# Batched matmul, one core: the first x in eight strided transfers, and each store queued behind y instead of between x and y

## The chip, the cores and the metric

One core of a Trainium2 chip runs the whole kernel. The metric is the device time of one execution, in microseconds (us). The kernel before takes 263.36 us, the median of three runs (263.03 to 263.59). Its profiled execution has a span of 261.6 us and a mean granted TensorE clock of 0.895.

## What is computed

```python
def setup_inputs():
    batch, m, k, n = 16, 512, 768, 1024
    return {
        "x": np.random.randn(batch, k, m).astype(np.float32),
        "y": np.random.randn(batch, k, n).astype(np.float32),
    }

def reference(x, y):
    return np.einsum('bkm,bkn->bmn', x, y).astype(np.float32)
```

There are sixteen independent products, each of a transposed 768x512 matrix with a 768x1024 matrix, all in float32. The kernel casts both inputs to bfloat16 before it multiplies. One batch needs 1.573 MB of x and 3.146 MB of y from HBM, and it writes 2.097 MB of output.

## The kernel before

One batch is called a round below. There are two buffers for x and two for y (`xs`, `ys` in float32), two slots of bfloat16 copies (`xb`, `yb`), two halves of PSUM (`ps`) and five output buffers (`ob`). All transfers are issued by SyncE, in program order, on one queue. A partition holds six consecutive rows of x or y, so that each partition's share is one contiguous piece of HBM (12 KB of x, 24 KB of y).

```python
    x_v = x.rearrange("b (p ko) m -> b p ko m", ko=KT)      # KT = 6, 128 partitions
    y_v = y.rearrange("b (p ko) n -> b p ko n", ko=KT)
    o_v = out.rearrange("b (p mo) n -> b p mo n", mo=MT)    # MT = 4
    LAG = 4
    NO = 5
    ...
    def wide_dma(key, dst, src, dram_rows, load):
        # the first transfer of a key is an ordinary one with 128 rows;
        # later ones are copies of it whose HBM side is widened:
        # 4 partitions' rows of x, or 2 of y, are one row
        if key not in made:
            made[key] = nc.sync.dma_start(dst, src)
            return made[key]
        ...
    def parts(b):
        return 2 if b in (15,) else 1            # the last y is cast in two halves

    nx = [sum(1 + parts(a) for a in range(b)) + 1 for b in range(B)]

    def store(b):
        if b < B - 2:
            nc.sync.wait_ge(groups, 2 * (b + 2))   # the matmuls of round b+1 are done
        else:
            nc.sync.wait_ge(outs, b - (B - 3))
        nc.sync.dma_start(o_v[b], ob[b % NO][:]).then_inc(so[b % NO], 16)

    for b in range(B):                             # SyncE
        i = b % 2
        if b >= 2:
            nc.sync.wait_ge(cast, nx[b - 2])                  # x of b-2 is cast
        wide_dma("x", xs[i][:], x_v[b], 4, True).then_inc(sx[i], 16)
        if LAG <= b < B - 1:
            store(b - LAG)
        if b >= 2:
            nc.sync.wait_ge(cast, nx[b - 2] + parts(b - 2))   # y of b-2 is cast
        wide_dma("y", ys[i][:], y_v[b], 2, True).then_inc(sy[i], 16)
        if b == B - 1:
            store(b - LAG)
    for b in range(B - LAG, B):
        store(b)
    ...
    for b in range(B):                             # VectorE
        i = b % 2
        n = 16 * (b // 2 + 1)
        if b >= 2:
            nc.vector.wait_ge(groups, 2 * (b - 1))
        nc.vector.wait_ge(sx[i], n)
        nc.vector.tensor_copy(xb[:, i], xs[i][:]).then_inc(cast, 1)
        nc.vector.wait_ge(sy[i], n)
        for h in range(parts(b)):
            ...   # cast of y, whole or in two halves, then_inc(cast, 1)
    ...
            # TensorE: 48 matmuls of 128x128 by 128x512 a round (4 mo x 6 kt x 2 nt);
            # after each half of mo: then_inc(groups, 1)
    ...
    for b in range(B):                             # ScalarE
        if b >= NO:
            nc.scalar.wait_ge(so[b % NO], 16 * (b // NO))
        for g in range(2):
            nc.scalar.wait_ge(groups, 2 * b + g + 1)
            cp = nc.scalar.copy(ob[b % NO][:, g * HB:(g + 1) * HB]..., ps[g][:])
            if b < B - 1:
                cp.then_inc(room, 1)
```

Of the kernel before, what the change touches and what calls it, by code (L numbers as in the profile page):

```python
# [1 line left out]

_os.environ.setdefault("NEURON_RT_ULTRASERVER_MODE", "4")

# [2 lines left out]

# [5 lines left out]


@with_exitstack
def kernel(
    ctx: ExitStack,
    tc: tile.TileContext,
    x: bass.AP,
    y: bass.AP,  # L20
    out: bass.AP,
):
    nc = tc.nc
    P = 128
    FP32 = mybir.dt.float32
    BF16 = mybir.dt.bfloat16

    B, K, M = x.shape
    _, _, N = y.shape
    KT = K // P  # L30
    MT = M // P
    NF = 512
    NT = N // NF

    x_v = x.rearrange("b (p ko) m -> b p ko m", ko=KT)
    y_v = y.rearrange("b (p ko) n -> b p ko n", ko=KT)
    o_v = out.rearrange("b (p mo) n -> b p mo n", mo=MT)

    LAG = 4
    NO = 5
    KH = KT // 2

    ctx.enter_context(tc.tile_critical())
    ec = ctx.enter_context
    xs = [ec(nc.sbuf_tensor(f"xs{i}", [P, KT, M], FP32)) for i in range(2)]
    ys = [ec(nc.sbuf_tensor(f"ys{i}", [P, KT, N], FP32)) for i in range(2)]
    xb = ec(nc.sbuf_tensor("xb", [P, 2, KT, M], BF16))
    yb = ec(nc.sbuf_tensor("yb", [P, 2, KT, N], BF16))  # L50
    ob = [ec(nc.sbuf_tensor(f"ob{i}", [P, MT, N], FP32)) for i in range(NO)]

    HB = MT // 2
    ps = [ec(nc.psum_tensor(f"ps{i}", [P, HB, NT, NF], FP32)) for i in range(2)]
    sx = [ec(nc.semaphore(f"sx{i}")) for i in range(2)]
    sy = [ec(nc.semaphore(f"sy{i}")) for i in range(2)]
    so = [ec(nc.semaphore(f"so{i}")) for i in range(NO)]
    cast = ec(nc.semaphore("cast"))
    ready = ec(nc.semaphore("ready"))
    room = ec(nc.semaphore("room"))  # L60
    groups = ec(nc.semaphore("groups"))
    idle = ec(nc.semaphore("idle"))
    outs = ec(nc.semaphore("outs"))


    made = {}
# [7 lines that stand above are left out]
        pat = mybir.BassSymbolicTensorAccessPattern  # L74
        widen = lambda a: a.rearrange("(q r) k m -> q (r k m)", r=dram_rows)
        plain = lambda a: a.rearrange("p k m -> p (k m)")
        s, d = (widen(src), plain(dst)) if load else (plain(src), widen(dst))
        return nc.sync.add_instruction(_copy.replace(
            made[key].ins, name=nc.get_next_instruction_name(),
            ins=(pat(ap=s.ap, dtype=s.dtype, bass_ap=s, is_dma=False),),  # L80
            outs=(pat(ap=d.ap, dtype=d.dtype, bass_ap=d, is_dma=False),),
            sync_info=None, ant_dge_precooked=False))


    def parts(b):
        return 2 if b in (15,) else 1
# [9 lines that stand above are left out]
            nc.sync.wait_ge(groups, 2 * (b + 2))  # L96
        else:
            nc.sync.wait_ge(outs, b - (B - 3))
        nc.sync.dma_start(o_v[b], ob[b % NO][:]).then_inc(so[b % NO], 16)

    for b in range(B):
        i = b % 2
        if b >= 2:
            nc.sync.wait_ge(cast, nx[b - 2])
        wide_dma("x", xs[i][:], x_v[b], 4, True).then_inc(sx[i], 16)
        if LAG <= b < B - 1:
            store(b - LAG)
        if b >= 2:
            nc.sync.wait_ge(cast, nx[b - 2] + parts(b - 2))
        wide_dma("y", ys[i][:], y_v[b], 2, True).then_inc(sy[i], 16)  # L110
        if b == B - 1:
            store(b - LAG)
    for b in range(B - LAG, B):
        store(b)


    for _ in range(60):
        nc.vector.sem_inc(idle, 1)
    for b in range(B):
        i = b % 2  # L120
        n = 16 * (b // 2 + 1)
        if b >= 2:
            nc.vector.wait_ge(groups, 2 * (b - 1))
        nc.vector.wait_ge(sx[i], n)
        nc.vector.tensor_copy(xb[:, i], xs[i][:]).then_inc(cast, 1)  # L125
        nc.vector.wait_ge(sy[i], n)
        for h in range(parts(b)):
            ks = slice(h * KT // parts(b), (h + 1) * KT // parts(b))
            nc.vector.tensor_copy(yb[:, i, ks], ys[i][:, ks]).then_inc(cast, 1)  # L129


    for b in range(B):
        nc.gpsimd.wait_ge(cast, nx[b]).then_inc(ready, 1)
        for h in range(parts(b)):
            nc.gpsimd.wait_ge(cast, nx[b] + h + 1).then_inc(ready, 2 // parts(b))


    x_w = xb[:].rearrange("p s k (j mo) -> p s k mo j", mo=MT)
    pe = OrderedEngineSet([nc.tensor.engine])
    with nc.Fori(0, B // 2, engines=pe):  # L140
        with nc.Fori(0, 2, engines=pe) as s:
            nc.tensor.wait_ge(ready, 2).then_inc(ready, -2)
            for mo in range(MT):
                g, m = divmod(mo, HB)
                if m == 0:
                    nc.tensor.wait_ge(room, 1).then_inc(room, -1)  # L146
                for kt in range(KT):
                    if mo == 0 and kt == KH:
                        nc.tensor.wait_ge(ready, 1).then_inc(ready, -1)
                    for nt in range(NT):  # L150
                        mm = nc.tensor.matmul(  # L151
                            ps[g][:, m, nt], x_w[:, bass.ds(s, 1), kt, mo],
                            yb[:, bass.ds(s, 1), kt, nt * NF:(nt + 1) * NF],
                            start=(kt == 0), stop=(kt == KT - 1))
                if m == HB - 1:
                    mm.then_inc(groups, 1)


    nc.scalar.nop().then_inc(room, 2)
    for _ in range(60):  # L160
        nc.scalar.sem_inc(idle, 1)
    for b in range(B):
# [4 lines that stand above are left out]
            cp = nc.scalar.copy(ob[b % NO][:, g * HB:(g + 1) * HB].rearrange("p m (t f) -> p m t f", f=NF),  # L167
                                ps[g][:])
            if b < B - 1:
                cp.then_inc(room, 1)  # L170
        if b == B - 2:
            nc.scalar.drain().then_inc(outs, 1)
    cp.then_inc(outs, 1)

    for i in range(NO):
        nc.sync.wait_ge(so[i], 16 * len(range(i, B, NO)))


# [1 line left out]
_INS = ['x', 'y']  # L180
_OUTS = [((16, 512, 1024), 'float32')]


# [23 lines left out]
```

## Time and profile before

| what | from the profile of before |
|---|---|
| TensorE (PE) busy | 190.3 us, 73% of the span, 768 matmuls |
| VectorE (DVE) busy | 82.0 us, 31%: casts of x at 1.76 us, of y at 3.36 us |
| ScalarE (ACT) busy | 61.1 us, 23%: copies out of PSUM at 1.87 us |
| moved by DMA | 75.50 MB read, 33.55 MB written |
| transfers | 16 of x, 16 of y, 16 stores |

The span is one execution as the hardware profiler recorded it. "Busy" is the time in which an engine had an instruction at work. A row of tenths cuts the span into 40 equal slices (6.54 us each) and gives the busy share of each slice as a digit. The DMA row is the mean share over the core's sixteen DMA engines, and the GB/s row is what they moved. An issue line of the transfer queue (SPq) gives the start and the length of the instruction that starts a transfer; the transfer itself comes later. The time from issue to landing ends when the completion semaphore is full.

### The profile page before, as it was taken

The numbers are of one execution on the slowest core, as the hardware profiler recorded it, in microseconds if no ns is written. First come the engines' busy times: TensorE is split into PE (matmuls) and PEld (weight loads), VectorE is DVE, ScalarE is ACT, GpSimd is POOL, SyncE is SP. The second block draws the span as 40 slices with busy tenths as digits, with TensorE's granted clock in tenths as the row PEclk, the third lists the DMA queues.
The fourth block names the chain that finished last, engine by engine and source line by source line (L and its number), as shares of the span: only waits on it lengthen the run. The fifth ranks groups of instructions, "written<-read, shape, count | busy, mean of one in ns | idle before, by whom it ended". The sixth has DMA issues, their size and how long they took to land. (4 is left out here: it accounts for less than half of the span.)

```text
span 261.6 us, 2506 instructions
## 1 busy us (share of the span) xinstructions
PE 190.3 (73%) x768; PEld 90.5 (35%) x768; DVE 82.0 (31%) x33; ACT 61.1 (23%) x33; POOL 0.2 (0%) x4
## 2 busy tenths in 40 slices
PE   0009999995494995939959499694968969499920
PEld 0004555552142352514425134252423525255500
DVE  0261734520705206052160612507043070525000
ACT  1000432343022022220312203222140222214220
POOL 0000000000000000000000000000000000000000
PEclk9999999999589597997989869799795989999995
DMA  6998999999999999989999998999999999999994
GB/s 263 442 485 376 474 398 451 328 466 436 403 443 378 461 443 428 448 371 469 406 476 401 403 504 366 451 466 423 408 393 491 388 441 453 406 411 428 426 391 180
DMA packets 4514, 109.07 MB, mean 417 GB/s; under 512 B 768, under 2 KB 768, under 8 KB 768
## 3 DMA queue, kind: packets, MB, share of 16 engines
q1 hardware_dynamic: 4512, 109.05, 97.9%
q14 instruction: 2, 0.02, 0.0%
HBM read 75.50 MB, written 33.55 MB: 417 GB/s over the span
## 5 line engine op out<-in xcount | busy, mean ns | idle before, releaser
L151 PE MATMUL ps<-yb,xb 128*128 x768 | 190.3, 414 | 59.8 <-PEq L146 59.7
L151 PEld LDWEIGHTS ps<-yb,xb 128*128 x768 | 90.5, 118 | 159.0 <-issue 93.9
L167 ACT COPY ob<-ps 128x2048 f32<-128x2048 f32 x32 | 59.8, 1869 | 185.5 <-PE ps L151 185.5
L129 DVE CAST yb<-ys 128x6144 bf16<-128x6144 f32 (+1 forms) x17 | 53.8, 3172 | 139.6 <-DMA ys<-in_y_dram 139.6
L125 DVE CAST xb<-xs 128x3072 bf16<-128x3072 f32 x16 | 28.2, 1760 | 18.0 <-DMA xs<-in_x_dram 15.0
L167 ACT ACT_TABLE_LOAD x1 | 1.3, 1283 | 5.3 <-issue 5.3
L191 POOL MEMSET const-bfloat16-1.0<- 128x1 bf16 x1 | 0.1, 102 | 0.0
L191 POOL MEMSET const-uint8-127<- 128x1 uint8 x1 | 0.1, 102 | 0.0
L191 POOL MEMSET const-float32-1.0<- 128x1 f32 x1 | 0.1, 99 | 0.0
L191 POOL MEMSET const-float32-0.0<- 128x1 f32 x1 | 0.1, 98 | 0.2 <-issue 0.2
## 6 DMA issues: line engine op xcount, KB each, us to landing
ys<-in_y_dram SPq DMA_DIRECT2D x16, 3072.0 KB, 28.2
out_dram<-ob SPq DMA_DIRECT2D x16, 2048.0 KB, 24.1
xs<-in_x_dram SPq DMA_DIRECT2D x16, 1536.0 KB, 29.8
```

Of the source, the lines that this page charges most:

```text
L125: nc.vector.tensor_copy(xb[:, i], xs[i][:]).then_inc(cast, 1)
L129: nc.vector.tensor_copy(yb[:, i, ks], ys[i][:, ks]).then_inc(cast, 1)
L151: mm = nc.tensor.matmul(ps[g][:, m, nt], x_w[:, bass.ds(s, 1), kt, mo], yb[:, bass.ds(s, 1), kt, nt * NF:(nt + 1) * NF], start=(kt == 0), ...
L167: cp = nc.scalar.copy(ob[b % NO][:, g * HB:(g + 1) * HB].rearrange("p m (t f) -> p m t f", f=NF), ps[g][:])
L191: nc = _bacc.Bacc("TRN2", target_bir_lowering=False, num_devices=1)
```

## The change

Two things are changed in the order of SyncE. The first x is no longer one transfer of 128 partitions but eight transfers of 16 partitions each: transfer c takes partitions c, c+8, c+16 and so on, so that each of the sixteen DMA engines has one partition in each of the eight. It is meant to let all engines start on the first data early. They all count on the semaphore of the first x buffer, which therefore stands 7 x 16 = 112 higher from then on. The first ordinary x transfer, which later ones are copies of, is now that of round 1. And each store now stands behind the y of its round in the queue, and no longer between x and y; this puts the operand that TensorE waits for ahead of the output, which nothing waits for until five rounds later.

```diff
+
+    x_first = x_v[0].rearrange("(a c) k m -> a c k m", c=8)
+    for c in range(8):
+        nc.sync.dma_start(xs[0][c::8], x_first[:, c]).then_inc(sx[0], 16)
     for b in range(B):
         i = b % 2
         if b >= 2:
             nc.sync.wait_ge(cast, nx[b - 2])
-        wide_dma("x", xs[i][:], x_v[b], 4, True).then_inc(sx[i], 16)
-        if LAG <= b < B - 1:
-            store(b - LAG)
+        if b > 0:
+            wide_dma("x", xs[i][:], x_v[b], 4, True).then_inc(sx[i], 16)
         if b >= 2:
             nc.sync.wait_ge(cast, nx[b - 2] + parts(b - 2))
         wide_dma("y", ys[i][:], y_v[b], 2, True).then_inc(sy[i], 16)
-        if b == B - 1:
+        if b >= LAG:
             store(b - LAG)
     for b in range(B - LAG, B):
         store(b)
@@
-        nc.vector.wait_ge(sx[i], n)
+        nc.vector.wait_ge(sx[i], n + (112 if i == 0 else 0))
```

## The prediction

> **What bounds the kernel now.** I read the page's slices and DMA totals first, because they show which resource is never free.
>
> ```profile
> span 261.6 us, 2506 instructions
> ...
> DMA  6998999999999999989999998999999999999994
> ...
> DMA packets 4514, 109.07 MB, mean 417 GB/s; under 512 B 768, under 2 KB 768, under 8 KB 768
> ...
> q1 hardware_dynamic: 4512, 109.05, 97.9%
> ```
>
> The DMA engines are busy for 97.9% of the span. Only the first slice (6) and the last (4) are clearly below 8. So any gain has to come from those two ends, or from a higher rate in between.
>
> For the rate I took the casts in order of time on VectorE, since a cast of y that waited for DMA starts when its data has landed. From round 11 on:
>
> ```profile
> 177.58 3.36 DVE L129 CAST yb<-ys 128x6144 bf16<-128x6144 f32 x1 [10.32 <-DMA ys<-in_y_dram]
> ...
> 193.38 3.36 DVE L129 CAST yb<-ys 128x6144 bf16<-128x6144 f32 x1 [10.33 <-DMA ys<-in_y_dram]
> ...
> 225.18 3.36 DVE L129 CAST yb<-ys 128x6144 bf16<-128x6144 f32 x1 [10.35 <-DMA ys<-in_y_dram]
> ...
> 236.15 3.43 DVE L129 CAST yb<-ys 128x3072 bf16<-128x3072 f32 x2 [5.46 <-DMA ys<-in_y_dram]
> ```
>
> From 177.58 to 225.18 are three rounds, so a round takes 15.87 us. It moves 1.573 + 2.097 + 3.146 = 6.816 MB, which makes 430 GB/s. TensorE needs 12.0 to 13.5 us of such a round, so it waits for y and not the reverse.
>
> Next I asked whether the queue ever runs dry. In the queue's own order of time, a steady round is:
>
> ```profile
> 183.09 0.47 SPq L72 DMA_DIRECT2D xs<-in_x_dram  x1
> 193.73 0.34 SPq L99 DMA_DIRECT2D out_dram<-ob  x1
> 196.77 0.47 SPq L72 DMA_DIRECT2D ys<-in_y_dram  x1
> ```
>
> The median time from issue to landing is 29.8 us for x and 28.2 us for y, nearly two rounds, so about 12 MB stands in the queue. A wait of SyncE on TensorE (130.2 us in all in the queue's waits) costs nothing while that much is queued.
>
> Last, the two ends. At the start, in windows of half a microsecond:
>
> ```profile
> 1.50:2.00 0.50, 0.00 (x0) 0.00 (x0) 0.00 (x0) 0.00 (x0) 0.00 (x0) 1.00 0.59 98
> 2.00:2.50 0.50, 0.00 (x0) 0.00 (x0) 0.00 (x0) 0.00 (x0) 0.00 (x0) 1.00 0.63 123
> 2.50:3.00 0.50, 0.00 (x0) 0.00 (x0) 0.00 (x0) 0.00 (x0) 0.00 (x0) 1.00 0.86 221
> 3.00:3.50 0.50, 0.00 (x0) 0.00 (x0) 0.00 (x0) 0.00 (x0) 0.00 (x0) 1.00 0.69 295
> 3.50:4.00 0.50, 0.00 (x0) 0.00 (x0) 0.00 (x0) 0.00 (x0) 0.00 (x0) 1.00 1.09 467
> ```
>
> The last column is GB/s. The rate climbs for 2 us, from 1.5 to 3.5, before it is full. In those 2 us 0.5 x (98+123+221+295) = 368 KB moved where 860 KB could have, a loss of 1.15 us. I read it as the sixteen engines getting their first work one after the other, the first at about 1.55 and the last near 3.4. At full rate an engine moves 27 GB/s and needs 3.66 us for its 98 KB of x, its eight rows; 3.4 + 3.66 = 7.06, and the first cast indeed starts at 7.11.
>
> At the end, issue plus landing time of the last five stores (windows of the transfer view) gives 241.05, 245.8, 250.7, 255.5 and 260.3. They are 4.8 us apart, and 2.097 MB in 4.8 us is 437 GB/s. So DMA holds the end as well, though the chain that ended last shows TensorE until 250.03 and the last copy until 251.93. The last store was issued at 251.9 and took 8.4 us. Alone it would take some 7.3 us (the first x took 6.1 us alone, of which 3.66 was data; 2.1 MB of data is 4.88 us, plus the same 2.4), so TensorE's chain has only about 1.1 us to spare.
>
> [...]
>
> [...] 48 transfers x 16 = 768, the profile's count of packets under 512 B.
>
> [...] Here the first issue is at 0.95 and the first packets are at about 1.55.
>
> [...] ten gaps of 2.4 to 6.4 us are each followed by 48 matmuls that take 12.0 to 13.5 us, but after the gap of 3.74 us before the last two rounds 96 of them took only 20.91 us.
>
> **The change part by part: the first x.** It removes one transfer and adds eight, 1.573 MB either way. An issue costs 0.34 us (stores) to 0.47 us (wide loads), with 0.05 us between; the first x took 0.39. I take 0.38 + 0.05 = 0.43 us, so the eight occupy SyncE from 0.95 to 4.4, where y of round 0 is issued (before: 1.39). An engine needs 12.3 KB / 27 GB/s = 0.457 us for each row, slightly more than the issue interval, so the rows follow each other without a hole. [...] it shrinks from 2 us to about 2/8 = 0.25, and the last engine starts at about 1.8. The x then lands at about 1.8 + 3.66 + 0.1 = 5.6 instead of 7.1.
>
> This gain is mostly lost again at once. The y of round 0 has 128 rows, and it makes its own climb: first engine at 4.4 + 0.6 = 5.0, last engine at 7.0. The engines have finished x at about 5.3 to 5.5, so the late half of them stand idle. Before, the last engine went over to y at 7.06; now at 7.0. Averaged over the engines, the change goes from (5.2 + 7.06)/2 = 6.1 to about 6.0. I book -0.1 to -0.4 us, and carry it undiminished to the end, because DMA is never idle after this.
>
> Further descriptors: x of round 1 is now the ordinary one (128 rows instead of 32), +96 packets, and seven more transfers make 112 completions; 4512 becomes 4720. That is 13 small extras an engine beside some 282, of the same bytes. I book +0.1 us.
>
> **The change part by part: the stores.** In eleven rounds, b = 4 to 14, two transfers change places: x, store, y becomes x, y, store. As a cycle this is one write of 4.88 us between 11 us of reads in either order, so the number of changes between reading and writing is the same and no byte is added. In the queue before the last five stores stands the same sum of work: y of round 15 should still land near 236.15. What moves is y against x: it lands one store, 4.9 us, earlier in its round. Then y lands 7.3 us behind its x, is cast 3.4 us later, and TensorE works from 11 to 24 us behind x, that is until 8 us into the next round. The new place of the store asks for that very round of matmuls just after the next y was issued, some 11 us into the round; it is met by then and the store goes out immediately. So SyncE no longer waits long for TensorE, and at least st, x, y and st, some 7 MB or 16 us, stay in the queue. The five output buffers also suffice: the store five rounds back lands about 4 us before the x whose matmuls' copy needs it, some 20 us early. Booked: 0.
>
> At the tail, round 14 now computes earlier (its y lands near 220.3), ends at 235 to 236, and TensorE then waits for y of round 15: 236.15 + 1.72 for half a cast + 0.57 of handing over = 238.4, instead of 239.6. With a slow restart it takes 12.2 (up to 13.4) us instead of 10.4: end at 250.6 (251.8) against 250.03. The last store would be issued at 252.5 (253.7), and alone end at 259.8 (261.0), against 260.3 set by DMA. Booked: +0.1 on average.
>
> Sum: -0.25 + 0.1 + 0 + 0.1, in effect nothing: 263.36 - 0.05, with the start perhaps doing better than I booked. I say 263.1 us.
>
> **The rivals.** One: the climb at the start is gone altogether, because issues of 16 rows are far cheaper than 0.43 us and y is queued early. Then up to the 1.15 us lost are won: 262.2. Against it speaks that all issues in the trace, of very different row counts, take 0.34 to 0.58 us. Two: the climb is a fixed delay for each engine, whatever the row count. Then x still lands near 7, y's issue at 4.4 does no harm, and the time is unchanged, 263.4. Three: the slow restart of TensorE at the tail takes the place of DMA as what ends last: +0.7, 264.0. Four: the place of stores against reads changes the rate. Rounds 5 to 7 take 16.2 to 16.7 us where later ones take 15.87, some 1.5 us in all, and I can't name what costs it; it may go or double: 261.9 to 264.9.
>
> **Range and chances.** The certain pieces lie within 0.5 us; the rivals reach from 262 to 264, and the three runs of before are themselves 0.56 apart. The range is 262.0 to 264.2. The border of 2% is 5.3 us away on either side. The gain is limited by 1.15 us at the start[...]; a loss would need the queue to run dry each round. So 0.97 within 2%, 0.015 for each side.
>
> **What would show it right or wrong.** Right: first cast at about 5.6, y of round 0 landing still near 14.8; in steady rounds the store's issue directly behind y's, the idle time before casts of y falling from 10.3 to some 5.5 and before casts of x rising by as much; rounds of 15.87 us; y of round 15 landing at about 236; the last five landings 4.8 us apart; 4720 packets. Wrong: issues of the small transfers much over or under 0.43 us, a DMA share under 0.97, rounds that differ from 15.87 by more than 0.1 us, or a last store issued after 253.

## The result and the profile after

The changed kernel takes 266.34 us (median of 4 runs, 265.98 to 266.74) beside 263.2 us for the kernel before. The ratio is 1.0117, with a 95% interval of 1.0097 to 1.0138. It is slower by 1.2%, or about 3.1 us. The prediction was 263.1 us with a range of 262.0 to 264.2: the change is within the 2% that was given a chance of 0.97, and outside the range.

The page of the changed kernel, its slices and DMA totals:

```profile
span 264.6 us, 2513 instructions
...
DMA  6999998999999899899999999899998999999993
GB/s 154 320 414 489 409 468 364 468 468 389 419 391 505 372 426 478 369 446 421 468 438 426 404 411 486 379 446 451 386 488 379 451 468 434 389 409 426 429 424 129
DMA packets 4722, 109.07 MB, mean 412 GB/s; under 512 B 880, under 2 KB 880, under 8 KB 880
...
q1 hardware_dynamic: 4720, 109.06, 97.7%
```

The same row of the kernel before:

```profile
GB/s 263 442 485 376 474 398 451 328 466 436 403 443 378 461 443 428 448 371 469 406 476 401 403 504 366 451 466 423 408 393 491 388 441 453 406 411 428 426 391 180
```

The engines are as busy as before (97.7%, before 97.9%), and the bytes are the same. But the second slice is a warning: a busy digit of 9 over 320 GB/s, where before it stood over 442. Engines that are busy but move less are not short of work: each packet takes longer (0.93 us instead of 0.457, counted below). The casts of VectorE in order of time show where the time goes:

```profile
11.02 1.76 DVE L128 CAST xb<-xs 128x3072 bf16<-128x3072 f32 x1 [11.02 <-DMA xs<-in_x_dram]
18.85 3.36 DVE L132 CAST yb<-ys 128x6144 bf16<-128x6144 f32 x1 [6.07 <-DMA ys<-in_y_dram]
...
191.32 3.36 DVE L132 CAST yb<-ys 128x6144 bf16<-128x6144 f32 x1 [5.57 <-DMA ys<-in_y_dram]
199.97 1.76 DVE L128 CAST xb<-xs 128x3072 bf16<-128x3072 f32 x1 [5.29 <-DMA xs<-in_x_dram]
207.19 3.36 DVE L132 CAST yb<-ys 128x6144 bf16<-128x6144 f32 x1 [5.46 <-DMA ys<-in_y_dram]
...
239.04 3.43 DVE L132 CAST yb<-ys 128x3072 bf16<-128x3072 f32 x2 [5.59 <-DMA ys<-in_y_dram]
```

The first two casts of the kernel before:

```profile
7.11 1.76 DVE L125 CAST xb<-xs 128x3072 bf16<-128x3072 f32 x1 [7.11 <-DMA xs<-in_x_dram]
15.03 3.36 DVE L129 CAST yb<-ys 128x6144 bf16<-128x6144 f32 x1 [6.16 <-DMA ys<-in_y_dram]
```

The first cast waits until 11.02 us where it waited until 7.11. The y of round 0 is 3.82 us later (18.85 against 15.03), and the last y 2.89 us later (239.04 against 236.15). In the middle a round still takes 15.87 us (207.19 - 191.32). So the loss is there before the first matmul.

The issues on SyncE's queue: the eight transfers and the y behind them, and a store behind y in a steady round.

```profile
0.95 5.04 SPq L104 DMA_DIRECT2D xs<-in_x_dram  x8
6.03 0.58 SPq L72 DMA_DIRECT2D ys<-in_y_dram  x1
...
194.71 0.47 SPq L72 DMA_DIRECT2D ys<-in_y_dram  x1
195.23 0.58 SPq L99 DMA_DIRECT2D out_dram<-ob  x1
```

In windows of the start, whose last two columns are the busy share of the DMA engines and GB/s:

```profile
2.00:2.50 0.50, 0.00 (x0) 0.00 (x0) 0.00 (x0) 0.00 (x0) 0.00 (x0) 1.00 0.53 147
2.50:3.00 0.50, 0.00 (x0) 0.00 (x0) 0.00 (x0) 0.00 (x0) 0.00 (x0) 1.00 0.77 246
3.00:3.50 0.50, 0.00 (x0) 0.00 (x0) 0.00 (x0) 0.00 (x0) 0.00 (x0) 1.00 1.32 393
...
5.00:6.00 1.00, 0.00 (x0) 0.00 (x0) 0.00 (x0) 0.66 (x1) 0.00 (x0) 1.00 0.98 209
...
7.00:8.00 1.00, 0.00 (x0) 0.00 (x0) 0.00 (x0) 0.00 (x0) 0.00 (x0) 1.00 1.00 205
8.00:9.00 1.00, 0.00 (x0) 0.00 (x0) 0.00 (x0) 0.00 (x0) 0.00 (x0) 1.00 0.97 197
```

A packet counts in the window in which it starts. By 3.5 us the changed kernel has started on 0.5 x (147 + 246 + 393) = 393 KB, hardly more than the 368 KB of before. From 5 to 9 us it moves 197 to 246 GB/s, about half of the 430 of a steady round, with a busy share near 1. A count of packets between 5 and 9 us says the same for one packet (transfer view of that window, changed kernel):

```profile
DMA packets 138, 0.86 MB, mean 214 GB/s; under 512 B 68, under 2 KB 68, under 8 KB 68
...
q1 hardware_dynamic: 137, 0.85, 100.8%
q14 instruction: 1, 0.01, 0.9%
```

The kernel before, in the same window:

```profile
DMA packets 111, 1.78 MB, mean 445 GB/s; under 512 B 16, under 2 KB 16, under 8 KB 16
```

Of the 138 packets 68 are completions (the packets under 512 B, of which the whole run has 880, 16 for each of its 55 transfers). That leaves 70, one of them an instruction fetch: 69 rows of 12 KB. Sixteen engines for 4 us are 64 engine-us, so a row takes 64 / 69 = 0.93 us. At the rate of a steady round (430 GB/s over 16 engines) it takes 0.457.

### The profile page after: what moved, and what is told of

It is laid out like the page before. It is cut to its first block, busy times and chain, and to the rows that moved or that the text cites. A ratio compares the mean times of both kernels' runs of the same rounds, so it can differ in the third digit from the quotient of the medians.

```text
span 264.6 us, 2513 instructions
## 1 busy us (share of the span) xinstructions
PE 187.7 (71%) x768; PEld 90.1 (34%) x768; DVE 82.0 (31%) x33; ACT 61.1 (23%) x33; POOL 0.2 (0%) x4
## 3 DMA queue, kind: packets, MB, share of 16 engines
q1 hardware_dynamic: 4720, 109.06, 97.7%
## 5 line engine op out<-in xcount | busy, mean ns | idle before, releaser
L154 PE MATMUL ps<-yb,xb 128*128 x768 | 187.7, 410 | 64.4 <-PEq L149 64.4
```

The source lines that it names most:

```text
L154: mm = nc.tensor.matmul(ps[g][:, m, nt], x_w[:, bass.ds(s, 1), kt, mo], yb[:, bass.ds(s, 1), kt, nt * NF:(nt + 1) * NF], start=(kt == 0), ...
```

## The experiments

The theory formed from this, A: the rate of a transfer goes with the partitions that it writes, and the sixteen with step 8 get half of it. What other sets of partitions would get was the author's estimate before the runs: the same half for sixteen with step 2, a quarter for sixteen neighbours, all of it for 128. No trace here shows what in the hardware would make it so; the runs show the rate of each set. The rivals: the order of stores costs (C), the rows read lie badly in HBM (D), or each transfer or its completion has a fixed cost (E).

**Which half of the change costs.** Two runs take one half of the change each. Order alone:

```diff
-    x_first = x_v[0].rearrange("(a c) k m -> a c k m", c=8)
-    for c in range(8):
-        nc.sync.dma_start(xs[0][c::8], x_first[:, c]).then_inc(sx[0], 16)
...
-        if b > 0:
-            wide_dma("x", xs[i][:], x_v[b], 4, True).then_inc(sx[i], 16)
+        wide_dma("x", xs[i][:], x_v[b], 4, True).then_inc(sx[i], 16)
...
-        nc.vector.wait_ge(sx[i], n + (112 if i == 0 else 0))
+        nc.vector.wait_ge(sx[i], n)
```

> The first x is one transfer as in the kernel before; only the stores stand behind y. Theory A (the whole loss is the start[...]): first cast at 7.1 us, time at or under that of before. From y of round 3 to y of round 15 the changed kernel took 187.19 us where before took 188.14, so if that 0.95 us comes from the order of stores the time is 262.4 us. Rival B (the order is neutral and the 0.95 us came from the later start): 263.3 us. Rival C (the order of stores is what costs): 265 us or more.

It took 262.56 us beside 262.72 us of before; ratio 0.9991, interval 0.9983 to 0.9999. Its first cast starts at 7.33 us. The eight transfers alone:

```diff
+        if LAG <= b < B - 1:
+            store(b - LAG)
...
-        if b >= LAG:
+        if b == B - 1:
             store(b - LAG)
```

> The first x comes in eight transfers as in the changed kernel; the stores stay between x and y. Theory A: first cast at 11.0 us, every later landing some 3.8 us later than before, 267.1 us if the order of stores is worth 0.95 us and 266.3 if it is neutral. Rival C (the order of stores costs): 264 us or less.

It took 266.37 us; ratio 1.0126 (1.0104 to 1.0149). Its first cast starts at 11.28 us. So the eight transfers are the whole loss, and C falls. The 0.95 us that the expectations hoped for from the order was mostly not there: it came from one profile of before, and the other kernels of the study spread from 185.33 to 187.22 us over the same stretch of rounds.

**Partitions, rows in HBM or fixed cost.** Here each of the eight transfers takes 16 neighbouring partitions:

```diff
-        nc.sync.dma_start(xs[0][c::8], x_first[:, c]).then_inc(sx[0], 16)
+        nc.sync.dma_start(xs[0][16 * c:16 * (c + 1)], x_v[0][16 * c:16 * (c + 1)]).then_inc(sx[0], 16)
```

> As the changed kernel, but each of the eight transfers takes 16 neighbouring partitions. Theory A [...] a 12 KB packet takes 4 x 0.46 = 1.84 us, x moves at 109 GB/s, first cast at about 17 us, 272 us in all. Rival D (rows 96 KB apart in HBM conflict): neighbouring rows are free of it, packets of 0.46 us, first cast at 7 to 8 us, 263 us. Rival E (a fixed cost for each of the eight transfers or their completions): as the changed kernel, first cast at 11.0 us, 266.3 us.

It took 270.68 us; ratio 1.0294 (1.0266 to 1.0322). First cast and packets between 5 and 9 us, the two views of this kernel in turn:

```profile
15.69 1.76 DVE L127 CAST xb<-xs 128x3072 bf16<-128x3072 f32 x1 [15.69 <-DMA xs<-in_x_dram]
```

```profile
DMA packets 77, 0.47 MB, mean 117 GB/s; under 512 B 39, under 2 KB 39, under 8 KB 39
...
q1 hardware_dynamic: 77, 0.47, 94.9%
```

In that window the engines were busy for 94.9% of 64 engine-us, so its 38 rows took 1.60 us each, 3.5 times 0.457. Sixteen neighbours get little more than half the rate of sixteen with step 8: 117 GB/s after 214. Eight transfers with eight completions each way, so E does not explain the difference, and rows that lie next to each other in HBM are no help, against D. That is a little better than the 4 x 0.457 expected, a factor that was the author's estimate, and the first cast came before the 17 us expected.

Step 2 within 32 partitions, another set of sixteen, and rows 24 KB apart in HBM in place of 96 KB:

```diff
-        nc.sync.dma_start(xs[0][c::8], x_first[:, c]).then_inc(sx[0], 16)
+        p = slice(32 * (c // 2) + c % 2, 32 * (c // 2 + 1), 2)
+        nc.sync.dma_start(xs[0][p], x_v[0][p]).then_inc(sx[0], 16)
```

> As the changed kernel, but each of the eight transfers takes 16 partitions with step 2 out of 32 neighbouring ones. Theory A [...] packets of 0.93 us, first cast at 11.0 us, 266.3 us. Rival D (distance of rows in HBM, 24 KB in place of 96 KB): first cast between 7 and 11 us. Rival E (fixed cost for each transfer): 11.0 us, 266.3 us too; it is told from A by the run with neighbouring partitions.

It took 266.25 us (1.0098 to 1.0153 of before), first cast at 11.00, and 220 GB/s between 5 and 9 us. So sixteen partitions with step 2 and sixteen with step 8 (214 GB/s) get nearly the same rate.

The sharpest cut between what is read and what is written: the rows of the changed kernel, written to 16 neighbouring partitions.

```diff
-        nc.sync.dma_start(xs[0][c::8], x_first[:, c]).then_inc(sx[0], 16)
+        nc.sync.dma_start(xs[0][16 * c:16 * (c + 1)], x_first[:, c]).then_inc(sx[0], 16)
```

> As the changed kernel in what it reads (16 rows of x with step 8 for each of the eight transfers), but each transfer writes them to 16 neighbouring partitions; so x of round 0 lies in another order of partitions than its y, and the product of round 0 is another one, with the same amount of work. Theory A [...]: the partitions written decide[...], packets of 1.84 us, first cast at 15.7 us as with neighbouring partitions before, 270.7 us. Rival D (the rows read decide): packets of 0.93 us, first cast at 11.0 us, 266.3 us.

It took 270.26 us (1.0265 to 1.0302). First cast:

```profile
15.15 1.76 DVE L128 CAST xb<-xs 128x3072 bf16<-128x3072 f32 x1 [15.15 <-DMA xs<-in_x_dram]
```

The same rows are read as in the changed kernel, and the time is within 0.5 us of that of the neighbouring partitions. The partitions written decide this difference of 3.9 us, and D falls. (The fourth combination, neighbouring rows written with step 8, was not run.)

**Eight transfers over all partitions.** Each takes all 128 partitions and an eighth of the columns:

```diff
-        nc.sync.dma_start(xs[0][c::8], x_first[:, c]).then_inc(sx[0], 16)
+        piece = slice(384 * c, 384 * (c + 1))
+        nc.sync.dma_start(x_land[:, piece], x_first[:, piece]).then_inc(sx[0], 16)
```

(`x_land` and `x_first` are the flat views of the buffer and of x.)

> As the changed kernel, but each of the eight transfers takes all 128 partitions and an eighth of the columns (pieces of 1.5 KB). Theory A: [...] first cast at 7.3 to 8.3 us, 263 us. Rival E (a fixed cost for each of eight transfers and their completions): first cast at 11.0 us, 266.3 us.

It took 263.16 us; ratio 1.0009 (0.9993 to 1.0025). The total is that of A. The start is not:

```profile
9.68 1.76 DVE L130 CAST xb<-xs 128x3072 bf16<-128x3072 f32 x1 [9.68 <-DMA xs<-in_x_dram]
```

The first cast lies between the two expectations, and 331 GB/s moved between 5 and 9 us. Its y of round 0 was 2.0 us later than before (17.06), and most of that was made up later. So this run does not clear E at the start: whether the eight transfers or the pieces of 1.5 KB slowed it was not separated. What E cannot explain is that the same eight transfers take 3.9 us more when only the partitions written are changed, as above, and 1.4 us less when only their order is, as below.

**The same eight in another order.** One of c = 0 to 3 and one of c = 4 to 7 by turns:

```diff
-    for c in range(8):
+    for c in (0, 4, 1, 5, 2, 6, 3, 7):
         nc.sync.dma_start(xs[0][c::8], x_first[:, c]).then_inc(sx[0], 16)
```

> As the changed kernel, but the eight transfers go in the order c = 0, 4, 1, 5, 2, 6, 3, 7. [...] Theory A, if the engines stay in step within one transfer: first cast at 11.0 us as in the changed kernel, 266.3 us. Theory A, if two transfers overlap in an engine: first cast between 7.5 and 10.5 us, 263 to 265.8 us. Rivals D and E (rows read, fixed cost): 11.0 us.

It took 264.9 us; ratio 1.0069 (1.0039 to 1.0099). First cast, and the packets between 5 and 9 us:

```profile
10.24 1.76 DVE L128 CAST xb<-xs 128x3072 bf16<-128x3072 f32 x1 [10.24 <-DMA xs<-in_x_dram]
```

```profile
DMA packets 157, 1.14 MB, mean 285 GB/s; under 512 B 78, under 2 KB 78, under 8 KB 78
```

285 GB/s in place of 214 with nothing changed but the order of the eight. As D and E were put, neither gives that. That window includes the first of y. Between 4 and 7 us there are only rows of x:

```profile
DMA packets 117, 0.74 MB, mean 246 GB/s; under 512 B 57, under 2 KB 57, under 8 KB 57
...
q1 hardware_dynamic: 117, 0.74, 100.7%
```

These 60 rows took 48.3 engine-us, 0.81 us each in place of 0.93, and the x lands 0.8 us sooner. First cast and total lie in the range that the expectation gave for transfers which overlap in an engine; whether they do was not shown.

**Fewer transfers, of more partitions each.** Four of 32 partitions with step 4, and two of 64 with step 2:

```diff
-    x_first = x_v[0].rearrange("(a c) k m -> a c k m", c=8)
-    for c in range(8):
-        nc.sync.dma_start(xs[0][c::8], x_first[:, c]).then_inc(sx[0], 16)
+    x_first = x_v[0].rearrange("(a c) k m -> a c k m", c=4)     # or 2
+    for c in range(4):
+        nc.sync.dma_start(xs[0][c::4], x_first[:, c]).then_inc(sx[0], 16)
...
-        nc.vector.wait_ge(sx[i], n + (112 if i == 0 else 0))
+        nc.vector.wait_ge(sx[i], n + (48 if i == 0 else 0))     # or 16
```

> As the changed kernel, but the first x comes in four transfers of 32 partitions with step 4[...]. Theory A[...]: packets of 0.46 us, first cast at about 6.5 us, 262.2 us. Theory A, if each engine is given two neighbours of the list (p and p+4): [...] packets near 0.93 us at first, first cast between 8 and 11 us, 263.5 to 266.3 us. Rival E (a fixed cost for each transfer): half of what eight transfers cost, first cast at 9 us, 264.5 us.

> As the changed kernel, but the first x comes in two transfers of 64 partitions with step 2[...]. Theory A[...]: first cast at about 6.8 us, 262.3 us. Theory A, if each engine is given four neighbours of the list[...]: between 7 and 11 us, 263 to 266.3 us. Rival E (a fixed cost for each transfer): a quarter of what eight transfers cost, first cast at 8 us, 263.5 us.

Four took 262.87 us (0.9994 to 1.0013), two 262.74 us (0.9986 to 1.0002). First casts at 8.26 and 7.52 us, neither earlier than the 7.11 of the one transfer of before. Two transfers move at full rate, 472 GB/s between 5 and 9 us (before 445); four begin below it (307 GB/s between 4.5 and 6.5 us, and 381 between 5 and 9). That lies between the two forms of A which the expectations gave; how the two partitions are dealt to an engine was not settled. No split of the first x won anything over one transfer, so what costs the first 2 us is not cured by smaller transfers.

**Order alone, again.** No edit beside the first run of it.

> The kernel with one first transfer and the stores behind y, once more: if its order of stores is worth a tenth of a per cent it is again below the kernel before (262.5 us beside 262.8), with an interval below 1; if the first comparison was chance, the interval holds 1.

It took 262.37 us beside 262.68; ratio 0.9978 (0.9969 to 0.9988). Both comparisons lie below 1, so the order behind y is worth 0.1 to 0.2%, and the kernel with one first transfer and the stores behind y is, by that little, faster than the kernel before. What makes the gain was not tested.

## Why the prediction was wrong, point by point

- **What bounds the kernel** was right: DMA, from the first packet to the last. The last three stores were issued at 239.12, 241.06 and 254.02 us and landed 14.5, 17.5 and 9.3 us later, at 253.6, 258.6 and 263.3. That is still one store's worth of data apart, so that a delay at the start had nowhere to vanish.
- **The step that failed** is in "the first x": "An engine needs 12.3 KB / 27 GB/s = 0.457 us for each row". It measured 0.93 with step 8, and 1.60 with neighbouring partitions. The rate was taken from transfers over 128 partitions and used for 16 partitions with step 8, as if an engine's rate were its own. How many engines such a transfer gets was asked, and not whether they keep their rate on these partitions. The first cast was 3.9 us late where -0.1 to -0.4 were booked. Eight rows at 0.93 instead of 0.457 would be 3.8 us of it, but so close a match is luck. By the packet records of the two traces the 128 rows took 6.85 us on each engine in place of 4.21, so 2.6 us more (the kernel before has slow rows too, at its start); the first row starts 0.4 us later (2.37 against 1.98), the cast follows the end of the last row by 0.85 us in place of 0.37, and the remaining 0.4 us lie between the rows. Two transfers of 64 partitions with step 2 cost nothing measurable (ratio 0.9994).
- **The issue**: 0.43 us expected, (6.03 - 0.95) / 8 = 0.635 us measured for step 8, and 0.46 for neighbouring partitions (eight in 3.64 us). Beyond the first issue (0.62 us in place of 0.39) it did not matter: the eighth ended at 5.99 us and y's at 6.6, when x still had 4 us to go.
- **The climb** was not cut by smaller transfers. The changed kernel alone does not tell (393 KB against 368 KB by 3.5 us, but under a halved rate); the splits that cost nothing in total (ratios 1.0004 and 0.9994) do: 344 KB with four, 357 KB with two. That a transfer of an eighth of the rows would climb in an eighth of the time was the author's estimate. Nor was the climb what the prediction took it for, engines that get their first work between 1.55 and 3.4 us. The transfer view of the kernel before from 1.8 to 2.7 us, which counts a packet where it starts:

```profile
DMA packets 14, 0.17 MB, mean 191 GB/s; under 512 B 0, under 2 KB 0, under 8 KB 0
...
q1 hardware_dynamic: 14, 0.17, 95.3%
```

Fourteen rows have started by 2.7 us, the sixteenth at 2.78, and the fourteen take 13.7 engine-us, 0.98 us each and not 0.457. So slow first rows make much of the climb; why they are slow stays open. The first row starts at 1.98 us, which is 1.0 us after the start of its issue and 0.6 us after its end (1.34): the 0.6 us that the prediction counted from the start of the issue (0.95 to 1.55) fits only if it is counted from its end. The last engine's start at 1.8 us, the climb of y at 5.0 to 7.0, and with them the booked gain, all went under in the halved rate. The first cast expected at 5.6 came at 11.02.

- **The extra packets** were counted right (4720). The 880 under 512 B are 55 transfers x 16 completions, which agrees with sixteen engines for each small transfer; the sixteen rows of the first are all under way at once (the last starts 0.46 us after the first, and none takes less than 0.458).
- **The stores** were right in every sign: from round 10 on idle time before casts of y of 5.5 to 5.6 us (expected 5.5, before 10.3), before casts of x 5.2 to 5.3 (before 0.4), rounds of 15.8 to 16.0 us, the store issued 0.5 us behind y. The order booked as 0 measured -0.1 to -0.2%. Rounds 5 to 7 still took 16.1 to 16.5 us, so what rival four could not name neither went nor doubled.
- **The tail**: the last store went out at 254.02, later than the 253 named as a sign against. But it is the start's delay that put it there. The last round of matmuls took 10.72 us, not 12.2, and the last store waited for DMA (9.3 us to land), so the rival of the slow restart did not come in. It would not have mattered: of the two runs of order alone one has a last round of 12.22 us and the other of 10.72, and their spans are 260.5 and 260.6.
- **"Carry it undiminished to the end"** was right within the noise. Beside the kernel before, 3.8 to 3.9 us at the first y become 3.1 to 3.3 us at the end by the ratios 1.0117 and 1.0126, but the runs of that kernel alone spread from 262.15 to 263.84 us. A closer partner of the changed kernel is order alone, which has the same order of stores. The first and the last y in its second run:

```profile
15.04 3.36 DVE L128 CAST yb<-ys 128x6144 bf16<-128x6144 f32 x1 [6.12 <-DMA ys<-in_y_dram]
...
235.14 3.43 DVE L128 CAST yb<-ys 128x3072 bf16<-128x3072 f32 x2 [5.45 <-DMA ys<-in_y_dram]
```

Against these the changed kernel is 3.8 us late at the first y (18.85) and 3.9 at the last (239.04), and the kernel with neighbouring partitions is 8.4 us late at both (23.44 and 243.54). It is no rule, though: with pieces of columns 2.0 us at the first y became 0.2 at the last (235.33), and why stays open.

- **The rivals** were all about the climb, the tail and the mix of reads and writes. None let the new transfers themselves be slow while their engines looked busy, which is why the range was too narrow upwards.

## What to carry to other kernels

A transfer cut into pieces must be judged by which partitions each piece writes, not only by how many engines it has: here pieces of sixteen partitions with step 8 moved at half of the steady 430 GB/s (214), and pieces of sixteen neighbours at little more than a quarter (117). If DMA is busy and the GB/s are half, look at the time of one packet before you look for missing work. Where DMA bounds the kernel from first to last, a few us lost in the first load can arrive whole at the end (3.8 us here), though a later round may make some of it up (1.8 of 2.0 us with pieces of columns). Moving a store in a queue that is never empty was worth a tenth of a per cent or two.

## What was not expected of the hardware

- A row of 12 KB took 0.93 us with step 8 and 1.60 us with neighbouring partitions, while the engines' busy share stayed at 1.01 and 0.95: the profile counts the longer time of a row as busy time, whatever it goes into.
- The order of the eight transfers matters even though they are issued one behind the other on one queue: 266.34 us in the order 0 to 7, 264.9 us with c = 0 to 3 and c = 4 to 7 by turns, and rows of 0.81 us in place of 0.93. What makes the difference was not shown.
- From one issue of 16 partitions to the next SyncE needed 0.635 us with step 8 and 0.46 us for neighbouring ones; the issue of the one transfer of all 128 took 0.39.
